# Expert outputs with tokens on partitions and 512 feature columns, and operands placed at the two ends of the on-chip memory

## The chip, the cores and the metric

One core of one Trainium2 chip runs the whole program. Engines are named as the profile names them: PE (TensorE matmul), PEld (its weight load), DVE (VectorE), ACT (ScalarE), POOL (GpSimd), SP (SyncE, which issues nearly all DMAs). The metric is the device time of one execution in microseconds; lower is better.

## The reference: two transformer blocks

256 tokens of 1,024 features go through two blocks in float32. The part that the change touches most is the feed-forward part of the first block, a mixture over 16,384 experts, each with one input row `u` and one output row `v`:

```
s = q . sub_keys;  pick 16 experts for each of 8 heads of each token, gate = softmax(best_s)
u_sel = u[expert];  v_sel = v[expert]
act = gelu(einsum('nd,ned->ne', hx, u_sel))
return einsum('ne,ned->nd', gate * act, v_sel)
```

Around it stand a block with selected attention, pooling branches and `w_out`, and a second block (a recurrent branch, a sparse attention, and a gated feed-forward of width 3,072). The rest is products of a 1,024-wide activation with weight matrices.

## The kernel before, in words

All large products run in float32r with both operands split in two: `x = h + l`. `h` is a rounded copy (ACT), `l` the rest (DVE or POOL), and a product is the sum of three matmuls, h·h, h·l and l·h. Weights arrive in units of 128 x 1,024 float32 (512 KB, one DMA on SP into one of four `raw` buffers). `weights()` hands out a unit and `prefetch()` keeps up to four ready: ACT writes `wh` (L166), DVE or POOL `wl` (L167). The order of units is one list, `stream`, from the first projection to the last one (`w1`, `wup1`, `wout1`, `wpq`, 128 of `u`, 128 of `v`, `w2`, `wup2`, `wout2`, `wff`, `wdn`), so PE goes from one stage to the next on weights that are already split. A unit's `wh` and `wl` stand in a *room*, and a pattern of letters says which: `w` is two pairs of buffers that live through the kernel, the other letters are places free in one stage only. In the u stage the pattern is `wwcc` (units 2 to 60), from the 64th `v` on it is `d`, and from `w2` to the end `wwe`.

Activations lie with features on partitions. `mm3` (L190) multiplies a unit with them: the weight block is loaded into PE (128x128), and 256 tokens stream past (the *moving* operand). A unit is 24 matmuls of 256 columns.

The experts are computed densely. **u stage** (128 units): `h2` (two halves of 128x8x256) streams past each unit, and gelu goes to `actA` or `actB`. After 64 units a second piece of work runs along: `gate_batch` builds for 8 tokens the 0/1 matrices of the chosen experts (four to five DVE operations, `eqa`, `a2`, `b8`), PE multiplies them (16 short matmuls, L797), and DVE multiplies the result into the activations (L805). **v stage** (128 units): ACT and DVE split two rows of activations into `pr` (h and l, L849 and L850), and L854 multiplies: the `v` block of 128 experts x 128 features is loaded, 256 tokens stream:

```
for d in range(8):
    for n, (wl, al) in enumerate(((0, 0), (0, 1), (1, 0))):
        mm = T.matmul(vo[d // 2][:, d % 2], (u.l if wl else u.h)[:, d], pr[al][:, i % 2], ...)
```

The sum of all 128 units stays in four banks of PSUM (`vo`, features on partitions). The first 58 units share the stage with the second half of the gate batches, and every eighth later unit with one `ada` product on DVE. After the last unit DVE adds `vo` into `x` chunk by chunk (L890), ACT and DVE split it into `hb` (L268, L269), and PE starts the first three units of `w2` on each chunk as it comes.

Where tiles lie is decided by pools that grow from the left (low bytes of a partition) or from the right. In the program before, in bytes of a partition: `w` rooms 47,264 to 63,648; `hb` and `mix2` 63,648 to 80,032; `h2` 80,288 to 96,672, and later `pr` in the same place; `oh` and `hf` 94,368 to 110,752; `c` rooms 147,424 to 163,808; `d` rooms (`spare`) 163,808 to 188,384; `ff` 163,808 to 212,960; `hh` and `hl` 212,832 to 229,344; `e` room 221,152 to 229,344. These tiles start 32 bytes past a multiple of 64. *Near* below means under 131,072, *far* above. Rows of activations are 1,024 bytes long, but those of `hh` and `hl` 1,032.

Of the kernel before, what the change touches and what calls it, by code (L numbers as in the profile page):

```python
# [58 lines left out]
def tile_kernel(ctx: ExitStack, tc: tile.TileContext, I, out):  # L59
    nc = tc.nc  # L60
    V, S, G, T = nc.vector, nc.scalar, nc.gpsimd, nc.tensor

    const = ctx.enter_context(tc.tile_pool(name="const", bufs=1))
    rawp = ctx.enter_context(tc.tile_pool(name="rawp", bufs=4))
# [210 lines left out]
    def load_c(wpool_):  # L275
        t = wpool_.tile([128, 1024], F32, name="cb", bufs=1)
# [61 lines left out]
    with ExitStack() as ph:  # L338
# [3 lines left out]
        wpx = pool(hst, "wpx", 2, side="right")  # L342
# [6 lines left out]
        rooms["a"], rooms["b"] = Room(6, wps), Room(2, wpx)  # L349
# [295 lines left out]
        hst = ExitStack()  # L645
        h2p = pool(hst, "h2p", side="left")
# [125 lines left out]
        def gate_batch(hf, act, n0, pg):  # L772
# [10 lines left out]
            a2 = pab.tile([128, 8, 2, 64], F16, name="a2")  # L783
# [4 lines left out]
            b8 = pab.tile([128, 8, 128], BF, name="b8")  # L788
# [23 lines left out]
        for i in range(64):  # L812
            if i == 0:
                pactA = pool(rst, "pactA", side="right")
                actA = [(0, pactA.tile([128, 24, 256], F32, name="actA0", tag="A0")),
# [20 lines left out]
        hst.close()  # L836
        upst.close()
        pp = pool(lst, "pp", 2, side="left")
        vst = ExitStack()
        pv = pool(vst, "pv", side="right", space=PSUM)  # L840
        vo = [pv.tile([128, 2, 256], F32, name=f"vo{i}") for i in range(4)]
        cb = load_c(pp)
        n0 = 0
        for i in range(128):
            u = weights("v", i)
            if i % 2 == 0:
                src = row(actA if i < 64 else actB, i % 64, 2)
                pr = (pp.tile([128, 2, 256], F32R, name="prh"), pp.tile([128, 2, 256], F32R, name="prl"))
                S.activation(pr[0], src, AF.Copy)  # L849
                V.tensor_tensor(pr[1], src, pr[0].bitcast(F32), OP.subtract)  # L850
            first = None
            for d in range(8):
                for n, (wl, al) in enumerate(((0, 0), (0, 1), (1, 0))):
                    mm = T.matmul(vo[d // 2][:, d % 2], (u.l if wl else u.h)[:, d], pr[al][:, i % 2],  # L854
                                  start=(i == 0 and n == 0 and d % 2 == 0),
                                  stop=(i == 127 and n == 2), skip_group_check=True)
                    if i == 0 and n == 0:
                        if d % 2 == 0:
                            first = mm
                        else:  # L860
                            tc.add_manual_dep(mm.ins, first.ins.name, no_sync(), reason="bank start")
# [676 lines left out]
```

## Time and profile before

| | |
|---|---|
| median of 3 runs | 1599.18 us (1594.93 to 1600.08) |
| profiled execution, its own time | 1595.43 us |
| its span in the trace | 1593.0 us |
| PE busy | 1539.8 us, 97%, 13,278 matmuls |
| PE weight loads | 1498.1 us, 94% |
| DVE / ACT / POOL busy | 1278.1 / 834.4 / 211.3 us |
| HBM read | 278.97 MB, 176 GB/s over the span |

A matmul's end in the trace is modelled and successive ones overlap, so a busy PE is not a PE at its peak: what a matmul costs in a stream is read from the distance between starts. In a timeline row such as `1561.77 1.12 PE ... x8` the first number is the start of the first of eight, and the next row's start minus it, over eight, is that distance.

### The profile page before, as it was taken

The numbers are of one execution on the slowest core, as the hardware profiler recorded it, in microseconds if no ns is written. First come the engines' busy times: TensorE is split into PE (matmuls) and PEld (weight loads), VectorE is DVE, ScalarE is ACT, GpSimd is POOL, SyncE is SP. The second block draws the span as 40 slices with busy tenths as digits, with TensorE's granted clock in tenths as the row PEclk, the third lists the DMA queues.
The fourth block names the chain that finished last, engine by engine and source line by source line (L and its number), as shares of the span: only waits on it lengthen the run. The fifth ranks groups of instructions, "written<-read, shape, count | busy, mean of one in ns | idle before, by whom it ended". The sixth has DMA issues, their size and how long they took to land.

```text
span 1593.0 us, 32813 instructions
## 1 busy us (share of the span) xinstructions
PE 1539.8 (97%) x13278; PEld 1498.1 (94%) x13278; DVE 1278.1 (80%) x2437; ACT 834.4 (52%) x1451; POOL 211.3 (13%) x156
## 2 busy tenths in 40 slices
PE   4999998999999999999999999988999999999999
PEld 3989998999999999999999999987888889999999
DVE  8889899984788887999856656888977666799963
ACT  3555563445444445434444444566776664576642
POOL 0100136895000000000000000125000000111100
PEclk9999999999999999999999999989999999999999
DMA  8678543655555555545466666544333335555554
GB/s 312 242 251 289 173 147 134 207 173 190 164 168 162 170 169 176 167 165 170 162 211 211 200 212 218 191 164 133 128 105 110 96 120 170 175 185 186 186 195 123
DMA packets 78215, 283.19 MB, mean 178 GB/s; under 512 B 8680, under 2 KB 9968, under 8 KB 77808
## 3 DMA queue, kind: packets, MB, share of 16 engines
q1 hardware_dynamic: 78064, 281.10, 53.3%
q8 instruction: 104, 1.70, 0.5%
q14 instruction: 47, 0.39, 0.1%
HBM read 278.97 MB, written 2.10 MB: 176 GB/s over the span
## 4 chain that ended last, share of the span: by engine, by line
PE 74%; DVE 6%; ACT 1%; issue 1%; DMA 0%; POOL 0%; ACTq 0%; POOLq 0%; DVEq 0%
PE mm L190 43%; PE vo L854 22%; PE gt L797 2%; DVE wl L167 2%; PE npo L1295 2%; PE pgt L1022 1%; PE npo L1298 1%; PE phd L1062 1%; DVE ri L1088 1%; PE npt L1286 0%; ACT wh L166 0%; DVE ri L1078 0%; DVE xt L992 0%; DVE hrr L946 0%; DVE eq L721 0%
## 5 line engine op out<-in xcount | busy, mean ns | idle before, releaser
L166 ACT ACTIVATE wh<-raw 128x1024 fp32r<-128x1024 f32 x409 | 432.5, 1060 | 471.4 <-PE mm L190 245.8
L167 DVE TENSOR_TENSOR wl<-raw,wh 128x1024 fp32r<-128x1024 f32 x359 | 447.8, 1249 | 104.0 <-ACT wh L166 102.4
L854 PE MATMUL vo<-prh,spare 128*128 128x256 f32 x1024 | 181.1, 281 | 0.0
L854 PEld LDWEIGHTS vo<-prh,spare 128*128 128x128 f32 x1024 | 158.1, 190 | 0.0
L190 PE MATMUL mm<-h2h,wl 128*128 128x256 f32 x1024 | 143.6, 283 | 5.7 <-DVE wl L167 5.7
L854 PE MATMUL vo<-prh,wh 128*128 128x256 f32 x512 | 146.7, 288 | 0.2 <-ACT prh L849 0.2
L190 PE MATMUL mm<-h2h,wh 128*128 128x256 f32 x1024 | 146.3, 286 | 0.0
L854 PE MATMUL vo<-prl,wh 128*128 128x256 f32 x512 | 144.5, 283 | 0.1
L854 PE MATMUL vo<-prh,wl 128*128 128x256 f32 x512 | 144.3, 283 | 0.2 <-DVE wl L167 0.2
L256 POOL TENSOR_TENSOR r<-r,sq 128x256 f32<-128x256 f32 x18 | 14.6, 809 | 978.0 <-DVE kh L960 606.7
L190 PE MATMUL mm<-h2l,wh 128*128 128x256 f32 x1024 | 144.0, 284 | 0.0
L854 PE MATMUL vo<-prl,spare 128*128 128x256 f32 x512 | 143.9, 281 | 0.0
L167 POOL TENSOR_TENSOR wl<-raw,wh 128x1024 fp32r<-128x1024 f32 x50 | 134.8, 2717 | 66.8 <-ACT wh L166 39.7
L190 PEld LDWEIGHTS mm<-h2h,wl 128*128 128x128 f32 x1024 | 131.8, 192 | 6.3 <-DVE wl L167 6.3
L190 PEld LDWEIGHTS mm<-h2l,wh 128*128 128x128 f32 x1024 | 132.3, 192 | 0.0
L190 PEld LDWEIGHTS mm<-h2h,wh 128*128 128x128 f32 x1024 | 131.2, 191 | 0.2
L167 DVE TENSOR_TENSOR spare<-raw,spare 128x1024 fp32r<-128x1024 f32 x64 | 78.4, 1225 | 65.5 <-ACT spare L166 65.5
L166 ACT ACTIVATE spare<-raw 128x1024 fp32r<-128x1024 f32 x64 | 67.8, 1059 | 92.3 <-PE vo L854 89.5
L854 PEld LDWEIGHTS vo<-prl,wh 128*128 128x128 f32 x512 | 98.0, 191 | 0.2 <-DVE prl L850 0.2
L854 PEld LDWEIGHTS vo<-prh,wl 128*128 128x128 f32 x512 | 97.8, 191 | 0.4 <-DVE wl L167 0.4
L854 PEld LDWEIGHTS vo<-prh,wh 128*128 128x128 f32 x512 | 97.8, 191 | 0.3 <-ACT prh L849 0.3
L854 PEld LDWEIGHTS vo<-prl,spare 128*128 128x128 f32 x512 | 96.1, 188 | 0.0
(419 smaller groups left out, 3270.5 us busy)
## 6 DMA issues: line engine op xcount, KB each, us to landing
raw<-in_u_dram SPq DMA_DIRECT2D x128, 512.0 KB, 3.6
raw<-in_v_dram SPq DMA_DIRECT2D x128, 512.0 KB, 3.6
raw<-in_w_dram SPq DMA_DIRECT2D x86, 512.0 KB, 4.3
raw<-in_wada_dram SPq DMA_DIRECT2D x48, 512.0 KB, 4.9
raw<-in_wff_dram SPq DMA_DIRECT2D x48, 512.0 KB, 4.3
raw<-in_wup_dram SPq DMA_DIRECT2D x27, 512.0 KB, 3.6
raw<-in_wdn_dram SPq DMA_DIRECT2D x24, 512.0 KB, 4.4
raw<-in_wout_dram SPq DMA_DIRECT2D x16, 512.0 KB, 3.7
```

What stands on the lines that cost most here:

```text
L166: S.activation(u.h, t, AF.Copy)
L167: (G if n in on_pool and on_pool[n](i) else V).tensor_tensor(u.l, t, u.h.bitcast(F32), OP.subtract)
L190: T.matmul(ps, (u.l if wl else u.h)[:, s], a[al][:, k], start=start and n == 0, stop=stop and n == len(seq) - 1)
L256: eng.tensor_tensor(tot, tot, sq, OP.add)
L797: mm = T.matmul(ps[:, t], b8[:, t], a2[:, t, s], start=(t == 0 and s == 0), stop=(s == 1), skip_group_check=True)
L854: mm = T.matmul(vo[d // 2][:, d % 2], (u.l if wl else u.h)[:, d], pr[al][:, i % 2], start=(i == 0 and n == 0 and d % 2 == 0), stop=(i == 1 ...
L1022: T.matmul(ps[:pn], w[:kn, idx % 8, :pn], a[:kn, i], start=(j == 0 and n == 0), stop=(j == len(ins) - 1 and n == 2))
L1062: T.matmul(phd, cw[hf][:, l], cb[:, 8 * hf + l], start=(hf == 0 and l == 0), stop=(hf == 1 and l == 7))
L1088: V.tensor_tensor_scan(ri[:, m], ra[:, m], xc[:, m], 0.0, op0=OP.mult, op1=OP.add)
L1295: T.matmul(po[64 * s:64 * s + 64], vs[i // (b + 1)][:, i % (b + 1), 64 * g:64 * g + 64], pT[:, s, i], start=(i == 0), stop=False)
L1298: T.matmul(po[64 * s:64 * s + 64], vc[:15, g], ct[:15, 2 * hp + s], start=False, stop=True)
```

## The change

**v stage.** The operands change sides. Now 128 tokens of `pr` are loaded into PE, and 512 feature columns of `wh`, `wl` or `spare` stream past. A unit is 12 matmuls of 512 columns instead of 24 of 256, in the order of the terms. `vo` holds tokens on partitions. The products of the last two units are ordered so that the first 512 features are complete before the second. Then ACT and DVE copy `vo` to `vt` (two copies of 128x512 each), PE turns it in 16 transposes of 128x128 into the same banks, and L928 adds it to `x`.

**Places.** A pool `hot` of 16 KB at the far end (212,928 to 229,312) holds in turn the `b` rooms, `h2`, three sets of `pr`, `hb` and `mix2`. `oh` and `hf` move to 196,544 to 212,928, `ff` to 139,200 to 188,352. The `d` rooms move near (80,384 to 104,960), the `e` room too (63,744 to 71,936). The `c` rooms stay far (155,584 to 171,968), the `w` rooms near (47,360 to 63,744). Two pad tiles make these tiles start at multiples of 64 bytes. `a2` and `b8` become one tile, and the row `c` for the last `ada` products is loaded at the 64th unit of `v` into a buffer of that pool instead of at the start of the stage.

```
+    const.tile([128, 24], F32, name="near_pad")
+    far_pad.tile([128, 8], F32, name="far_pad")
...
+    hot = ctx.enter_context(tc.tile_pool(name="hot", bufs=1, reuse_waits="tile", side="right"))
+    def hot_acts(name):
+        t = hot.tile([128, 2, 8, 256], F32R, name=name, tag="hot")
+        return t[:, 0], t[:, 1]
...
+        pA0 = pool(lst, "pA0", side="left")
-        h2 = (h2p.tile([128, 8, 256], F32R, name="h2h"), h2p.tile([128, 8, 256], F32R, name="h2l"))
+        h2 = hot_acts("h2")
...
+        pv_ = hot.tile([128, 8, 2, 256], F32R, name="pr", tag="hot")
+        prs = [(pv_[:, 2 * n], pv_[:, 2 * n + 1]) for n in range(3)]
...
+        vo = [[pv.tile([128, 4, 128], F32, name=f"vo{b}{hf}") for hf in range(2)] for b in range(2)]
+        def v_products(halves):
+            for u, pr, i in held_v:
+                for n, (wl, al) in enumerate(((0, 0), (0, 1), (1, 0))):
+                    for b in range(2):
+                        for hf in halves:
+                            T.matmul(vo[b][hf], pr[al][:, i % 2, b * 128:b * 128 + 128],
+                                     (u.l if wl else u.h)[:, 4 * hf:4 * hf + 4],
+                                     start=(i == 0 and n == 0), stop=(i == 127 and n == 2))
...
+            held_v.append((u, pr, i))
+            if i < 126:
+                v_products(range(2))
+                held_v.clear()
+            elif i == 127:
+                for hf in range(2):
+                    v_products([hf])
...
-                spare = pactA.tile([128, 3, 2, 8, 128], F32R, name="spare", tag="A0")
+                spare = pA0.tile([128, 3, 2, 8, 128], F32R, name="spare", tag="A0")
-        rooms["e"] = Room(1, pool(ctx, "wpe", 1, side="right"))
+        rooms["e"] = Room(1, pool(ctx, "wpe", 1, side="left"))
-        hb = (b2h.tile([128, 8, 256], F32R, name="hbh", tag="hbh"),
-              b2h.tile([128, 8, 256], F32R, name="hbl", tag="hbl"))
+        hb = hot_acts("hb")
...
+        for hf in range(2):
+            S.activation(vt[0][:, 4 * hf:4 * hf + 4], vo[0][hf], AF.Copy)
+            V.tensor_copy(vt[1][:, 4 * hf:4 * hf + 4], vo[1][hf])
+        def turned(m):
+            t = vo[m % 4 // 2][m // 4][:, 2 * (m % 2):2 * (m % 2) + 2]
+            for b in range(2):
+                T.transpose(t[:, b], vt[b][:, m], ident)
+            return t.rearrange("p b n -> p (b n)")
+        yo = [turned(m) for m in range(4)]
         for m in range(8):
+            if m < 4:
+                yo.append(turned(4 + m))
-            xm = V.scalar_tensor_tensor(x[:, m], vo[m // 2][:, m % 2], ada[:, 40 + m:41 + m], x[:, m],
+            xm = V.scalar_tensor_tensor(x[:, m], yo[m], ada[:, 40 + m:41 + m], x[:, m],
...
-        b2o = pool(ctx, "b2o", side="left")
+        b2o = pool(ctx, "b2o", side="right")
```

PE in the middle of the v stage, before (each `vo` is one bank that holds two chunks of 128 features; a unit is eight such triples):

```order
L854 MATMUL vo_8091<-prh,wh 128x256
L854 MATMUL vo_8091<-prl,wh 128x256
L854 MATMUL vo_8091<-prh,wl 128x256
L854 MATMUL vo_8091<-prh,wh 128x256
L854 MATMUL vo_8091<-prl,wh 128x256
L854 MATMUL vo_8091<-prh,wl 128x256
L854 MATMUL vo_8092<-prh,wh 128x256
```

And PE with the change, one whole unit (`vo_8020` and `vo_8021` are the two feature halves of the first 128 tokens, `vo_8022` and `vo_8023` of the others; `pr` stands for its h and its l):

```order
L865 MATMUL vo_8020<-wh,pr 128x512
L865 MATMUL vo_8021<-wh,pr 128x512
L865 MATMUL vo_8022<-wh,pr 128x512
L865 MATMUL vo_8023<-wh,pr 128x512
L865 MATMUL vo_8020<-wh,pr 128x512
L865 MATMUL vo_8021<-wh,pr 128x512
L865 MATMUL vo_8022<-wh,pr 128x512
L865 MATMUL vo_8023<-wh,pr 128x512
L865 MATMUL vo_8020<-wl,pr 128x512
L865 MATMUL vo_8021<-wl,pr 128x512
L865 MATMUL vo_8022<-wl,pr 128x512
L865 MATMUL vo_8023<-wl,pr 128x512
```

Twelve long matmuls stand where 24 short ones stood, and `wl` is first needed at the ninth of twelve instead of at the third of 24.

DVE at the end of the v stage, before (the `x` rows add the expert output, the `hbl` rows split it):

```order
L890 SCALAR_TENSOR_TENSOR x<-vo_8091,ada,x 128x256 x2
L890 SCALAR_TENSOR_TENSOR x<-vo_8092,ada,x 128x256
L958 MEMSET nought 128x4
L1058 COPY cb<-vec 128x16 x2
L960 CAST kh<-nought 128x4
L167 TENSOR_TENSOR wl<-raw,wh 128x1024
L269 SCALAR_TENSOR_TENSOR hbl<-x,vec,hbh 128x256 x3
```

And DVE with the change:

```order
L179 TENSOR_TENSOR wl<-raw,wh 128x1024 x2
L915 COPY vt_11234<-vo_8022 128x512
L915 COPY vt_11234<-vo_8023 128x512
L928 SCALAR_TENSOR_TENSOR x<-vo_8020,ada,x 128x256 x2
L928 SCALAR_TENSOR_TENSOR x<-vo_8022,ada,x 128x256
L281 SCALAR_TENSOR_TENSOR hb<-x,vec,hb 128x256
```

Two copies stand ahead of the first `x`, and the split of a weight unit that stood between `x` and `hbl` stands ahead of both. On PE, 16 transposes (L921) stand between the last product of `v` and the first of `w2`.

## Rows read from the trace of the kernel before

**Rows 1.** Windows: each engine's busy time (operations), granted clock, DMA share, GB/s

```profile
288.00:405.00 117.00, 116.98 (x985) 116.98 (x986) 86.83 (x205) 55.44 (x84) 88.46 (x33) 1.00 0.59 194
414.00:614.00 200.00, 200.00 (x2035) 198.62 (x2034) 166.90 (x287) 85.21 (x127) 0.00 (x0) 1.00 0.51 167
616.00:802.00 186.00, 185.87 (x1897) 184.46 (x1896) 174.22 (x294) 79.46 (x91) 0.00 (x0) 1.00 0.51 168
802.00:998.00 196.00, 195.84 (x1660) 195.62 (x1660) 117.40 (x134) 93.32 (x108) 0.00 (x0) 1.00 0.67 212
1013.00:1300.00 287.00, 272.87 (x2109) 251.13 (x2108) 231.30 (x471) 196.51 (x479) 34.82 (x33) 0.97 0.38 124
1300.00:1384.00 84.00, 83.53 (x690) 81.19 (x689) 57.84 (x85) 42.98 (x69) 4.48 (x6) 1.00 0.53 176
1384.00:1523.00 139.00, 138.56 (x1161) 138.31 (x1160) 129.85 (x216) 95.93 (x146) 17.74 (x24) 1.00 0.57 183
```

**Rows 2.** Chain that ended last, v stage: start, us, what

```profile
640.77 5.82 PE vo L854 x48
646.59 0.48 PE gt L797 x16
```

**Rows 3.** Tile vo: duration min/median/max, first and last start

```profile
L854 PE MATMUL vo<-prh,spare x1024: 281/281/283, 817.2 to 998.0; 128*128 128x256 f32 x171
```

**Rows 4.** Timeline of PE, last stage, units in `e`, `w`, `w`, `e`

```profile
1561.77 1.12 PE L190 MATMUL mm<-ffh,wh 128*128 128x256 f32 x8
...
1564.65 1.07 PE L190 MATMUL mm<-ffh,wh 128*128 128x256 f32 x8
...
1567.37 1.07 PE L190 MATMUL mm<-ffh,wh 128*128 128x256 f32 x8
...
1570.09 1.12 PE L190 MATMUL mm<-ffh,wh 128*128 128x256 f32 x8
```

**Rows 5.** Timeline of PE, u stage, units in `w`, `c`, then `w`

```profile
340.30 1.12 PE L190 MATMUL mm<-h2h,wh 128*128 128x256 f32 x8
...
343.18 1.11 PE L190 MATMUL mm<-h2h,wh 128*128 128x256 f32 x8
...
348.83 1.12 PE L190 MATMUL mm<-h2h,wh 128*128 128x256 f32 x8
```

**Rows 6.** Timeline of PE, `wff` stage, a unit in `e`, then `w`

```profile
1451.32 1.11 PE L190 MATMUL mm<-hfh,wh 128*128 128x256 f32 x8
...
1454.15 1.12 PE L190 MATMUL mm<-hfh,wh 128*128 128x256 f32 x8
```

**Rows 7.** Timeline of PE, first projection, one unit in `w`, then the next

```profile
117.14 1.11 PE L190 MATMUL mm<-hh,wh 128*128 128x256 f32 x8
...
119.98 1.12 PE L190 MATMUL mm<-hh,wh 128*128 128x256 f32 x8
```

**Rows 8.** Timeline of PE at 114 us, three windows: plain float32, two passes a matmul

```profile
114.36 0.91 PE L507 MATMUL pl<-kk,q 64*128 64x256 f32 x3
...
114.36 1.13 PE L507 MATMUL pl<-kk,q 64*128 64x256 f32 x4
...
114.68 0.81 PE L507 MATMUL pl<-kk,q 64*128 64x256 f32 x3
```

**Rows 9.** Timeline of weight loads, ahead of matmuls of 2 columns

```profile
64.23 1.41 PEld L226 LDWEIGHTS ms<-blk,sq 128*128 128x128 f32 x12
65.57 0.19 PEld L190 LDWEIGHTS mm<-hh,wh 128*128 128x128 f32 x1
```

**Rows 10.** Timeline at the end of the v stage

```profile
996.19 1.27 DVE L890 SCALAR_TENSOR_TENSOR x<-vo,ada,x 128x256 f32<-128x256 f32 x3 [1.28 <-PE vo L854]
...
997.99 0.28 PE L854 MATMUL vo<-prh,spare 128*128 128x256 f32 x1
...
1000.68 0.39 PE L190 MATMUL mm<-hbl,wh 128*128 128x256 f32 x1 [2.05 <-DVE hbl L269]
```

**Rows 11.** Timeline of DVE, v stage: an operation of 128x512 from PSUM

```profile
704.42 0.69 DVE L805 SCALAR_TENSOR_TENSOR actB<-gt,actB 128x512 f32<-128x512 f32 x1 [0.54 <-PE gt L797]
```

More of the change, by code (lines that the diff above doesn't have):

```diff
@@ L348, in tile_kernel @@
         wps = pool(stp, "wps", 6, side="left")
-        rooms["a"], rooms["b"] = Room(6, wps), Room(2, wpx)
+        wpx = hot.tile([128, 2, 2, 8, 128], F32R, name="wpx", tag="hot")
+        rooms["a"] = Room(6, wps)
+        rooms["b"] = Room(2, pairs=[(wpx[:, n, 0], wpx[:, n, 1]) for n in range(2)])
         sqrt_next()
@@ L782, in gate_batch @@
                             i1b[:, sl, None].to_broadcast([128, 8, 32, 2]), OP.is_equal)
-            a2 = pab.tile([128, 8, 2, 64], F16, name="a2")
+            ab = pab.tile([128, 2, 1024], BF, name="ab")
+            a2 = ab[:, 1].bitcast(F16).rearrange("p (t s i) -> p t s i", t=8, s=2)
             for s in range(2):
@@ L835, in tile_kernel @@
                 n0 += 8
-        hst.close()
         upst.close()
-        pp = pool(lst, "pp", 2, side="left")
+        pv_ = hot.tile([128, 8, 2, 256], F32R, name="pr", tag="hot")
+        prs = [(pv_[:, 2 * n], pv_[:, 2 * n + 1]) for n in range(3)]
         vst = ExitStack()
         pv = pool(vst, "pv", side="right", space=PSUM)
-        vo = [pv.tile([128, 2, 256], F32, name=f"vo{i}") for i in range(4)]
-        cb = load_c(pp)
+        vo = [[pv.tile([128, 4, 128], F32, name=f"vo{b}{hf}") for hf in range(2)] for b in range(2)]
+        cb = None
         n0 = 0
+        held_v = []
+        def v_products(halves):
[6 more added lines that the diff above has]
+                                     start=(i == 0 and n == 0), stop=(i == 127 and n == 2))
         for i in range(128):
@@ L847, in tile_kernel @@
                 src = row(actA if i < 64 else actB, i % 64, 2)
-                pr = (pp.tile([128, 2, 256], F32R, name="prh"), pp.tile([128, 2, 256], F32R, name="prl"))
+                pr = prs[i // 2 % 3]
                 S.activation(pr[0], src, AF.Copy)
                 V.tensor_tensor(pr[1], src, pr[0].bitcast(F32), OP.subtract)
[L851 to L861, printed above, removed]
+            held_v.append((u, pr, i))
[5 more added lines that the diff above has]
+                    v_products([hf])
             if i < 64:
@@ L888, in tile_kernel @@
         los = []
+        vtp = pool(vst, "vtp", side="right")
+        vtp.tile([128, 4096], F32, name="gap")
+        vt = [vtp.tile([128, 8, 128], F32, name=f"vt{b}") for b in range(2)]
+        for hf in range(2):
[7 more added lines that the diff above has]
+        yo = [turned(m) for m in range(4)]
         for m in range(8):
-            xm = V.scalar_tensor_tensor(x[:, m], vo[m // 2][:, m % 2], ada[:, 40 + m:41 + m], x[:, m],
+            if m < 4:
+                yo.append(turned(4 + m))
+            xm = V.scalar_tensor_tensor(x[:, m], yo[m], ada[:, 40 + m:41 + m], x[:, m],
                                         op0=OP.mult, op1=OP.add)
@@ L1366, in tile_kernel @@
         yw = pool(ph, "yw", 2, side="right")
-        mix = (b2h.tile([128, 8, 256], F32R, name="mix2h", tag="hbh"),
-               b2h.tile([128, 8, 256], F32R, name="mix2l", tag="hbl"))
+        mix = hot_acts("mix2")
         for m in range(8):
```

13 lines of the change are left out of this document (6 added, 7 removed).

## The prediction

> **What bounds the kernel now.** [...] DVE comes close in the first v window (174.2 of 186 us) and in `wff` (129.9 of 139) [rows 1]. [...]
>
> [...] In the last stage, whose activations lie far, the three units from 1561.77 us on start at 1561.77, 1564.65, 1567.37 and 1570.09: 24 matmuls take 2.88 us where the weights lie far (120.0 ns each) and 2.72 us where they lie near (113.3 ns) [rows 4]. The other engines do the same work around all three. In the u stage, activations near, the unit with near weights takes 2.88 us (120 ns) and two with far weights 5.65 us (117.7 ns) [rows 5]. `wff`, activations near too, repeats it: 2.83 us with far weights, 117.9 ns [rows 6]. The second part of v, pr near and weights far, 64 units of 24 matmuls, runs at (998.0 - 817.2) / 1536 = 117.7 ns [rows 3]. So four cases: both near 120, both far 120, activations near and weights far 117.7, activations far and weights near 113.3.
>
> A weight load by itself, ahead of matmuls of two columns, takes (1.41 - 0.19) / 11 = 111 ns [rows 9]. That is nearly the whole distance at 256 columns. The nearest stream that lasts longer is plain float32 at 256 columns: the fourth pass adds 1.13 - 0.91 = 0.22 us to three, and the last two of three add (0.81 - 0.38) / 2 = 0.215 (a single one lasting 0.38 by 1.13 less three distances), so 216 ns; but the first pass of a pair takes 114.68 - 114.36 = 0.32 [rows 8]. I have no row of a 512-column float32r matmul.
>
> **The change, part by part.** (1) *512 columns.* The 3,072 matmuls of v become 1,536. [...] Bounds: 216 below; above, twice the short ones, 227 to 240 ns [rows 4, 5]. The first 58 units share PE with 32 gate batches of 0.48 us [rows 2]: 58 x 12 x 0.216 = 150.3, plus 15.4, plus the 3.6 that today's 186 holds over 58 x 24 x 0.120 + 15.4, is 169 us. But DVE has 174.2 us of work there, which the change leaves as it is, so it becomes the limit: I take 175, a gain of **11 us** and not 17 [rows 1]. The other 70 units: 70 x 12 x 0.216 = 181.4 against 196, gain **14.6**; DVE (117) and ACT (93) stay under it, and the DMAs, 0.67 of their time busy now, would go to 0.72 [rows 1].
>
> (2) *Activations far, weights near* (6.7 ns a matmul against both near, 4.4 against far weights). *u stage, second part*: 64 units, 1,523 matmuls in the window, x 6.7 = **10.2 us**; DVE's 166.9 of 200 still fits in 190 [rows 1]. *u stage, first part*, 288 to 405 us: half of the 41 units gain 6.7 ns, the half in `c` rooms, now far with `h2` far, loses 2.3 (120 against 117.7): 492 x 6.7 - 492 x 2.3 = **2.2 us**; POOL, 88.5 / 33 = 2.68 us per `wl`, stays just under a unit's mean of 2.80 [rows 1]. Before 288 us I count nothing: what streams there (`hh`, `hl`) was far before and stays so. *w2 stage*: 1,320 matmuls, two in three in `w` rooms (6.7) and one in three in the `e` room (4.4), make 7.8; DVE is busy 231 of 287 us there and PE waits for it in places, so I take **5**, between 0 and 7.8 [rows 1]. *wup2 and wout2*: 384 with `oh` and `mix2` at a mean of 5.9 ns gain 2.3; the 264 on `y`, near as before, lose 2.3 ns in the `e` room, 0.2: **2.1**. *wff*: 1,152 x 5.9 = **6.8**, which brings the window to 132 against DVE's 129.9: just under [rows 1]. *wdn*: 192 matmuls in the `e` room x 6.7 = **1.3** [rows 4]. Is far enough? The new place, from 212,928 up, was held only by `hh`, whose unit with near weights takes 2.84 us (118.3 ns) [rows 7]; its rows are 1,032 bytes apart, those of `h2`, `pr`, `hb` and `mix2` 1,024 as in `ff`, so I go by `ff`, with 118.3 as the other bound.
>
> (3) *Multiples of 64.* No row has both operands on one. All of 113, 118 and 120 are read 32 bytes past. [...] I take nothing.
>
> (4) *End of v.* Today 2.7 us pass from the last expert matmul to PE's first on `hbl`, 2.05 of them a wait [rows 10]. With the change DVE copies the second half (0.69, as an operation of 128x512 from PSUM takes [rows 11]), then three `x` (1.27 for three [rows 10]) and one `hb` (some 0.45, as `x`): 2.4 us and two passages between engines, about the same. The 16 transposes need 16 weight loads of 0.111 = 1.8 us [rows 9], inside that wait; without it they would cost their 1.8. The remaining `x` and `hb` come a little later than today, because today three `x` are done before the last matmul: **cost 1 us**, 0 to 4. What is queued behind the second copy on DVE is every `x`, and PE waits for these. Its late start delays nothing but the first three units of `w2`.
>
> (5) *The row `c`* is now loaded at the 64th unit, ahead of a `raw` load that already makes DVE wait; the `d` rooms hold three units ahead. One `a2`/`b8` tile instead of two keeps two buffers. `pr` has three sets for two. The `b` rooms, `h2`, `pr`, `hb`, `mix2` follow each other in one place, each after a stage that PE runs in order. I price these at 0; the cover is the units kept ready.
>
> Sum: 11 + 14.6 + 10.2 + 2.2 + 5 + 2.1 + 6.8 + 1.3 - 1 = **52.2 us** off the profiled execution's 1595.43, or 1543.2. That execution is 3.75 us under the median of 1599.18, so a median of about **1547**.
>
> **The rivals.**
>
> *Places do nothing for PE.* Then 113.3 comes from something else in the last stage. Left are 25.6 of (1) less 1: **1575**. The alternation inside one stage speaks against it [rows 4, 6]; `hh` at 118.3 speaks for a part of it [rows 7]. [...]
>
> [...]
>
> *Long streams cost more than 216.* At 227 the 70 units take 190.7 and the first 58 177: 40.9 us gained in all, **1558**. At 240 the 70 take 201.6 and the 58 take 186: 21 gained, **1578**.
>
> *Slower: the weight load is not hidden behind long streams.* The 0.32 us of a first float32 pass is 216 plus a load of about 107 [rows 8, 9]. Were every matmul of v like it, v would take 1536 x 0.32 + 19 = 511 us against 382, and the kernel **1700**. It decides from 254 ns on, where 1536 of them use up the other 26.6 us. Against it: at 256 columns the load is hidden today, or the distance would be over 200 ns [rows 3].
>
> *The change does not do what it says:* the waits of (5), or DVE in the two near-full stages, give back what PE saves, and the time is within a few us of today, **1595 to 1605**.
>
> **How the numbers follow.** Forecast (1540 to 1559) 0.58; alignment gives more 0.17; places do nothing 0.08; long streams at 227 to 240 0.08; given back 0.06; load not hidden 0.03. Within 0.3% of 1599, 4.8 us, is about what a measurement can't tell from no change. The first four cases are faster: 0.91. Given back divides 0.04 same and 0.02 slower, and the last adds 0.03: slower 0.05. The range reaches from 1524, the fast end of alignment, to 1577, which takes in "places do nothing" and most of the long streams; about 0.12 is left out.
>
> **What would show it.** L865's distance near 216 ns in the second part of v; 24 matmuls of `h2` on `w` rooms in 2.72 us or less, and 2.88 in `c` rooms; DVE filling the first part of v with PE waiting for it; the wait at the end of v about as long as today; `wff` with DVE over 0.95. Wrong would be: a distance over 227 ns in v, or `h2` at 118 to 120 in its new place.

## The result, and the profile after

| | before | after |
|---|---|---|
| median | 1599.4 us (1594.9 to 1600.1) | 1572.2 us (1571.4 to 1573.8) |
| ratio, 95% interval | | 0.984 (0.9822 to 0.9858) |
| profiled execution, its span | 1593.0 us | 1570.0 us |
| `u`, first to last start | 395.1 us | 390.4 us |
| `v` | 382.7 us | 369.3 us |
| last product of `v` to first of `w2` | 0.1 us | 2.1 us |
| `wff` | 138.4 us | 136.7 us |
| `wdn` | 66.7 us | 67.7 us |

The change is worth 27 us where 52 were forecast. The two profiled executions differ by 23.0 us in their spans, and the forecast was summed against the one of before. The windows by stage (columns as in [rows 1]) of the changed kernel:

```profile
414.00:608.00 194.00, 194.00 (x2060) 192.86 (x2060) 168.66 (x289) 85.32 (x129) 0.00 (x0) 1.00 0.55 176
611.00:799.00 188.00, 188.00 (x1232) 151.04 (x1230) 179.50 (x301) 85.76 (x100) 0.00 (x0) 1.00 0.54 175
799.00:978.00 179.00, 179.00 (x784) 146.87 (x783) 110.78 (x124) 86.65 (x98) 0.00 (x0) 1.00 0.70 227
1362.00:1498.00 136.00, 135.46 (x1150) 135.22 (x1149) 132.61 (x212) 91.70 (x145) 17.69 (x24) 1.00 0.58 186
```

PE fills these four stretches, or nearly, as it filled those of [rows 1], at a granted clock of 1.00, so what counts is the distance between starts. In v the tile's view (columns as in [rows 3]) gives it: from 804.0 to 979.6 us lie 767 steps, 228.9 ns each, where 216 were forecast.

```profile
L865 PE MATMUL vo<-spare,pr x768: 388/392/396, 804.0 to 979.6; 128*128 128x512 f32 x192
L865 PE MATMUL vo<-wh,pr x512: 388/392/502, 610.3 to 802.9; 128*128 128x512 f32 x171
```

For 256 columns I read PE's timeline: two units of `u` in `w` rooms and one in a `c` room (336 to 345 us), one unit late in `u`, and one unit of `wff`:

```profile
336.42 2.05 PE L202 MATMUL mm<-h,wh 128*128 128x256 f32 x16
...
339.25 2.05 PE L202 MATMUL mm<-h,wh 128*128 128x256 f32 x16
...
342.08 2.08 PE L202 MATMUL mm<-h,wh 128*128 128x256 f32 x16
...
344.96 1.24 PE L202 MATMUL mm<-h,wh 128*128 128x256 f32 x9
...
595.55 1.98 PE L202 MATMUL mm<-h,wh 128*128 128x256 f32 x16
...
598.27 1.98 PE L202 MATMUL mm<-h,wh 128*128 128x256 f32 x16
...
1402.70 1.10 PE L202 MATMUL mm<-hfh,wh 128*128 128x256 f32 x8
...
1405.52 1.10 PE L202 MATMUL mm<-hfh,wh 128*128 128x256 f32 x8
```

From one row shown to the next is a unit of 24 matmuls. At 336 us the `w` rooms take 2.83 us a unit (117.8 ns) and the `c` room 2.88 (120). At 595 us the same `w` rooms with the same `h2`, no address changed, take 2.72 (113.3). `wff` takes 2.82 to 2.83 throughout, and so does `wdn`, where `w` rooms had 2.72 before [rows 4]. So the places alone do not give 113.3.

The view of waits shows PE standing in the first part of `u` for splits that queue on DVE behind the top-k (us in total, times, longest), first before the change, then with it:

```profile
PE mm L190 <- DVE wl L167: 5.7, 3, 3.6
...
PE mm L202 <- DVE wl L179: 8.3, 3, 4.1
```

The end of v, in the timeline:

```profile
979.59 1.92 PEld L921 LDWEIGHTS vo<-ident,vt 128*128 128x128 f32 x16
...
980.02 0.69 DVE L915 COPY vt<-vo 128x512 f32<-128x512 f32 x1 [1.33 <-PE vo L865]
...
980.63 1.26 DVE L928 SCALAR_TENSOR_TENSOR x<-vo,ada,x 128x256 f32<-128x256 f32 x3
...
981.70 1.02 PE L202 MATMUL mm<-hb,wh 128*128 128x256 f32 x4
...
982.34 0.19 PEld L202 LDWEIGHTS mm<-hb,wh 128*128 128x128 f32 x1 [0.22 <-DVE hb L281]
```

The first product on the low half of `hb`, whose load is the last row, comes 2.8 us after the last product of v (979.56), against 2.7 before [rows 10]. The transposes fill what was a wait. The first product on the high half comes 2.1 us after it instead of 0.1.

### The profile page after: what moved, and what is told of

Same layout as the page of the kernel before. It is cut to its first block, busy times and chain, and to the rows that moved or that the text cites. A ratio compares the mean times of both kernels' runs of the same rounds, so it can differ in the third digit from the quotient of the medians.

```text
span 1570.0 us, 29771 instructions
## 1 busy us (share of the span) xinstructions
PE 1514.9 (96%) x11758; PEld 1404.7 (89%) x11758; DVE 1286.6 (82%) x2439; ACT 831.3 (53%) x1453; POOL 213.6 (14%) x156
## 5 line engine op out<-in xcount | busy, mean ns | idle before, releaser
L202 PE MATMUL mm<-h,wh 128*128 128x256 f32 x2048 | 263.8, 282 | 0.0
L202 PEld LDWEIGHTS mm<-h,wh 128*128 128x128 f32 x2048 | 249.5, 191 | 0.2
L865 PE MATMUL vo<-spare,pr 128*128 128x512 f32 x768 | 176.0, 391 | 0.0
L865 PEld LDWEIGHTS vo<-spare,pr 128*128 128x128 f32 x768 | 144.2, 188 | 31.6
L202 PE MATMUL mm<-h,wl 128*128 128x256 f32 x1024 | 141.9, 282 | 8.3 <-DVE wl L179 8.3
L202 PEld LDWEIGHTS mm<-h,wl 128*128 128x128 f32 x1024 | 129.9, 192 | 8.9 <-DVE wl L179 8.9
L202 PE MATMUL mm<-hb,wh 128*128 128x256 f32 x928 | 130.7, 287 | 0.6 <-ACT wh L178 0.2
L865 PE MATMUL vo<-wh,pr 128*128 128x512 f32 x512 | 130.8, 397 | 0.3 <-ACT pr L874 0.3
L202 PEld LDWEIGHTS mm<-hb,wh 128*128 128x128 f32 x928 | 117.6, 192 | 3.7 <-issue 1.4
L865 PEld LDWEIGHTS vo<-wh,pr 128*128 128x128 f32 x512 | 93.7, 188 | 19.0 <-ACT pr L874 0.4
```

Of the source, the lines that this page charges most:

```text
L202: T.matmul(ps, (u.l if wl else u.h)[:, s], a[al][:, k], start=start and n == 0, stop=stop and n == len(seq) - 1)
L865: T.matmul(vo[b][hf], pr[al][:, i % 2, b * 128:b * 128 + 128], (u.l if wl else u.h)[:, 4 * hf:4 * hf + 4], start=(i == 0 and n == 0), stop ...
```

## Experiments: what each part is worth

Three parts can be put in singly: the **turn** of v to 512 columns, the two **pads**, and the **places** (far activations, near rooms). Five kernels leave out one or two of them. `x_turn_only` is the kernel before with the new v stage:

```
-        vo = [pv.tile([128, 2, 256], F32, name=f"vo{i}") for i in range(4)]
+        vo = [[pv.tile([128, 4, 128], F32, name=f"vo{b}{hf}") for hf in range(2)] for b in range(2)]
...
+                            T.matmul(vo[b][hf], pr[al][:, i % 2, b * 128:b * 128 + 128],
+                                     (u.l if wl else u.h)[:, 4 * hf:4 * hf + 4],
```

> The kernel before with the 512-column v stage and its turning at the end alone; every place as before (pr near, w rooms near in the first part of v, spare far in the second). Kernel before: 1599.4 us, v 382.7 us. Theory 1 (a long matmul takes twice a short one on the same places): 240 ns in the first part, where both operands lie near, and 227 to 236 in the second; v 375 to 389 us, the end of v 2 us longer, total 1594 to 1607. Rival 2 (the long stream costs 229 ns wherever its operands lie): v 369 us as in the changed kernel, total 1586 to 1589.

`x_pads_only` is the kernel before with

```
+    const.tile([128, 24], F32, name="near_pad")
+    far_pad = ctx.enter_context(tc.tile_pool(name="far_pad", bufs=1, side="right"))
+    far_pad.tile([128, 8], F32, name="far_pad")
```

> The kernel before with the two pad tiles alone: all its tiles start at multiples of 64 bytes, in the order and the places of before. Kernel before: 1599.4 to 1600.5 us. Theory 1 (a multiple of 64 sets no distance of 256-column matmuls; only the rhythm that they fall into may change): u at 120, v at 120 and 117.7, total within 4 us of 1600. Rival 2 (alignment is worth what the changed kernel loses without the pads, 1584 against 1572, 12 us): total 1588 to 1592, with a shorter distance in v.

`x_turn_pads` has both of these edits:

> The kernel before with the 512-column v stage and the two pads, all places as before: what is missing to the changed kernel is the move of activations and rooms alone. The turn alone gave 1584.9 us, the pads alone 1591.4, the changed kernel 1572.2. Theory 1 (the places are worth little of their own, since 113.3 is only one of two rhythms of operands that lie apart, and the second part of u is the one long stretch that keeps it): v 366 to 370 us, u 393 to 397, total 1577 to 1582, so 5 to 10 us for the places. Rival 2 (the places carry the 25.6 us that the prediction gave them): total 1595 to 1600. Rival 3 (they carry nothing, turn and pads are all): 1571 to 1574.

`x_no_pads` takes the three pad lines out of the changed kernel:

> The changed kernel without its two pad tiles: every tile starts 32 bytes past a multiple of 64 again, the far and near places are kept to within 96 bytes. Theory 1 (a multiple of 64 does nothing for PE): the distances stay at 113.3 in the second part of u, 229 in v, 117.8 in wff, and the total within 3 us of 1572.2. Rival 2 (it does): the distance in the second part of u goes back to 117.7 to 120, total 1579 to 1583; or wff and wdn go to 113.3 as the last stage had before, total 1564 to 1567. DVE operations may change too: an operation of 128x2048 in the first part of u was 4.4 us before and 2.3 or 9.2 with the change.

`x_v256` undoes the turn in the changed kernel and keeps its places:

```
-                            T.matmul(vo[b][hf], pr[al][:, i % 2, b * 128:b * 128 + 128],
-                                     (u.l if wl else u.h)[:, 4 * hf:4 * hf + 4],
+                    mm = T.matmul(vo[d // 2][:, d % 2], (u.l if wl else u.h)[:, d], pr[al][:, i % 2],
```

> The changed kernel with the v stage as it was before (24 matmuls of 256 columns a unit, weights loaded, pr streams, no turning at the end), all places kept: pr far, weight rooms near. Changed kernel: 1572.2 us, v stage 369.3 us from its first matmul to its last. Theory 1 (the 512-column form brings nothing of its own: its 229 ns is twice a short matmul of operands that lie apart, and v became faster because pr moved away from the weights): 256 columns at 113.3 ns where a gate batch interrupts the stream and 113.3 to 117.8 ns where nothing does, so v takes 361 to 374 us, the 2 us between v and w2 go, total 1562 to 1577. Rival 2 (the long stream is what made v faster): 256 columns at 117.7 to 120 ns as before, v 378 to 383 us, total 1579 to 1584.

Measured (the ratio is to runs of the kernel before on the same chip; the last two columns are spans between first starts in one profile each):

| kernel | turn | pads | places | median, us | ratio (95%) | `u` | `v` |
|---|---|---|---|---|---|---|---|
| before | | | | 1599.4 | 1 | 395.1 | 382.7 |
| `x_turn_only` | x | | | 1584.9 | 0.992 (0.9891 to 0.995) | 397.2 | 368.4 |
| `x_pads_only` | | x | | 1591.4 | 0.9954 (0.9933 to 0.9974) | 395.9 | 376.3 |
| `x_turn_pads` | x | x | | 1586.8 | 0.9937 (0.9916 to 0.9958) | 397.8 | 371.8 |
| `x_no_pads` | x | | x | 1583.9 | 0.9909 (0.9874 to 0.9944) | 392.3 | 375.3 |
| `x_v256` | | x | x | 1575.5 | 0.9861 (0.983 to 0.9892) | 388.4 | 370.1 |
| after | x | x | x | 1572.2 | 0.984 (0.9822 to 0.9858) | 390.4 | 369.3 |

A few us between single profiles say little here: before the first product of `u`, which most of these edits do not touch, the profiles of all runs take between 217.7 and 224.3 us. The turn alone came near rival 2 (v at 368.4), the short matmuls on the new places as theory 1 had it (v at 370), and both runs on the pads on rival 2's side. The parts don't add. The turn is worth 13 us alone (0.8%) and nothing that can be told apart once pads and places are there (0.9861 against 0.984, intervals overlapping). In v each way of its own leads to about 369: `x_turn_only` has the places of before, `x_v256` the short matmuls of before. The reason shows in the tile's view of the second part of v, first `x_v256`, then `x_turn_only`:

```profile
L868 PE MATMUL vo<-pr,spare x1536: 276/276/387, 809.4 to 984.1; 128*128 128x256 f32 x192
```

```profile
L851 PE MATMUL vo<-spare,prh x512: 388/392/397, 809.1 to 984.6; 128*128 128x512 f32 x171
```

`x_v256` takes 1,535 steps in 174.7 us, 113.8 ns. Outside a few waits a unit there takes 2.72 us, 113.3 ns a matmul, and twice that is 226.7. So 512 columns save nothing over two good short matmuls; they save over the 117.7 to 120 ns of before.

The pads, priced at zero, are worth 7 us alone, nothing on top of the turn, and 11 on top of turn and places. The tile's view of the second part of v shows a part of why, first `x_no_pads`, then `x_turn_pads`, then `x_pads_only`:

```profile
L862 PE MATMUL vo<-spare,pr x768: 393/397/398, 807.5 to 986.5; 128*128 128x512 f32 x192
```

```profile
L854 PE MATMUL vo<-spare,prh x512: 393/394/394, 809.7 to 988.7; 128*128 128x512 f32 x171
```

```profile
L857 PE MATMUL vo<-prh,spare x1024: 275/276/281, 822.2 to 996.7; 128*128 128x256 f32 x171
```

With long matmuls a step takes 233.3 ns in `x_no_pads` and again 233.3 in `x_turn_pads`, against 228.9 both in the changed kernel and in `x_turn_only`. So with `pr` far and `spare` near the pads take 4.4 ns off a step, and with `pr` near and `spare` far they add 4.4: rival 2 of `x_turn_only`, 229 ns wherever the operands lie, does not hold in general. With short matmuls `x_pads_only` went from 117.7 [rows 3] to 113.7 on the mean. In `u` the distances changed places: without the pads the `w` units of the first part took 2.72 us and the second part ran at 117.8 ns, where the changed kernel has 2.83 us and 113.3. For 256 columns, then, 113.3 and 117.8 both occur with the pads and without them, and whether 32 bytes act by themselves there, or only something decides between the two, is not shown.

The places on top of turn and pads are worth 0.9937 less 0.984, 15 us, of 27.6 forecast: step (2) of the prediction sums to 27.6, and the 25.6 that rival 2 of `x_turn_pads` names is the forecast gain of the turn. The total of `x_turn_pads` hit none of its three expectations; it lies between theory 1, which gave the places 5 to 10 us, and rival 2, which gave them all.

## Experiment: the distances with nothing else running

`x_probe` adds blocks of 48 matmuls behind the last product of the changed kernel:

```
+        def probe(st, mv, n, reset, off=0, count=48):
+            ps = px.tile([128, 512], F32, name="pr0", tag="x")
+            for _ in range(3 * reset):
+                T.transpose(ps[:, :128], ident, ident)
+            for k in range(count):
...
+                T.matmul(ps[:, :n], st[:, 128 * (k % 8):128 * (k % 8) + 128], mv[:, a:a + n],
+                         start=(k == 0), stop=(k == count - 1))
```

> The changed kernel with 18 blocks of 48 matmuls (the first of 96) added behind its last product, when no other engine works: operands near or far in all four ways, 256 and 512 columns, some blocks after three short transposes, some right behind another block, two with the moving operand 32 bytes further on. Their results go nowhere, the output is that of the changed kernel, and the total says nothing. Theory 1 (PE alone makes the distances: same side 120, apart 113.3 after short matmuls and 117.8 behind a block at 120; 512 columns twice that, 226 to 240): the blocks show these numbers with all other engines idle. [...]

One window of it shows PE alone (columns as in [rows 1]), and PE's timeline the blocks. In these rows `hfh` and `mix` lie far and `wh` near; the first name is the moving operand, and a row with `wh` alone has both near.

```profile
1592.30:1597.00 4.70, 4.70 (x43) 4.70 (x41) 0.00 (x0) 0.00 (x0) 0.00 (x0) 1.00 0.00 0
```

```profile
1569.16 11.04 PE L1475 MATMUL pr<-hfh,wh 128*128 128x256 f32 x96
1580.04 0.49 PE L1472 MATMUL pr<-ident 128*128 128x128 f32 x3
1580.29 5.70 PE L1475 MATMUL pr<-hfh,wh 128*128 128x256 f32 x48
1585.82 5.92 PE L1475 MATMUL pr<-hfh,mix 128*128 128x256 f32 x48
1591.58 5.82 PE L1475 MATMUL pr<-hfh,wh 128*128 128x256 f32 x48
1597.24 0.49 PE L1472 MATMUL pr<-ident 128*128 128x128 f32 x3
1597.48 5.90 PE L1475 MATMUL pr<-hfh,wh 128*128 128x256 f32 x48
1603.22 5.91 PE L1475 MATMUL pr<-wh 128*128 128x256 f32 x48
1608.97 5.63 PE L1475 MATMUL pr<-hfh,wh 128*128 128x256 f32 x48
1614.44 0.49 PE L1472 MATMUL pr<-ident 128*128 128x128 f32 x3
...
1649.95 11.45 PE L1475 MATMUL pr<-hfh,wh 128*128 128x512 f32 x48
1661.24 0.49 PE L1472 MATMUL pr<-ident 128*128 128x128 f32 x3
1661.49 11.16 PE L1475 MATMUL pr<-hfh,mix 128*128 128x512 f32 x48
1672.49 0.49 PE L1472 MATMUL pr<-ident 128*128 128x128 f32 x3
...
1683.73 11.15 PE L1475 MATMUL pr<-wh,mix 128*128 128x512 f32 x48
1694.72 0.49 PE L1472 MATMUL pr<-ident 128*128 128x128 f32 x3
```

Start to next start: apart 10.88 / 96 = 113.3 ns; both far 5.76 / 48 = 120.0; then the same operands as in the first block 5.66 / 48 = 117.9. Both near gave 120 too. At 512 columns both far takes (11.00 - 0.31) / 47 = 227.4, the 0.31 being the first one behind the transposes. Apart it takes 10.99 / 48 = 229.0 with the loaded operand far and the moving one near, as in the changed kernel, and (11.29 - 0.32) / 47 = 233.4 the other way round, as in `x_turn_pads`. The windows read inside seven of these blocks (256 columns apart, both far and both near; 512 apart and both far) show DVE, ACT and POOL at 0.00 us and a DMA share of 0.01 at most, so the distances of these seven need no other engine. Theory 1 stands for the distances, not for what sets them. With the moving operand 32 bytes further on, one block of 256 columns apart took 119.8, and one of 512 took 232.3.

Two rows say what the forecast missed. Apart has two **rhythms**, 113.3 and 117.9, for the same operands. What turns the one into the other does not follow theory 1: behind the first block at 120 (1585.82) came 117.9, behind the second (1603.22) came 5.47 / 48 = 114.0, and the blocks behind three transposes (1580.29 and 1597.48, without their first matmul of 0.20 us 113.4 and 117.9) kept the rhythm of the block ahead of the transposes. And long streams want the opposite of short ones: one side 227, apart 229 to 233.5.

## Experiments: the rhythm inside the kernel

`x_reset` puts three transposes ahead of the third unit of `wff`, `after_again` is the changed kernel once more:

```
+                if m == 1 and i == 0:
+                    for _ in range(3):
+                        T.transpose(ps[:, :128], ident, ident)
```

> The changed kernel with three transposes of 128x128 into the output of the third unit of wff ahead of its first product, which overwrites them; nothing else. In the changed kernel wff and wdn run at 117.8 ns with activations far and weights near, the second part of u at 113.3 with the same places, each unit there starting after some short matmuls. Theory 1 (operands that lie apart allow two rhythms, 113.3 and 117.8 ns, and which one PE keeps is set by what it did just before; short matmuls set it to 113.3): wff from the third unit on and wdn run at 113.3, 1,104 + 576 matmuls x 4.5 ns less 0.4 us: 7 us less, total 1565. Rival 2 (the distance belongs to the addresses): 117.8 stays, total 1572 to 1573.

> The changed kernel once more, unchanged, for a second profile and its time beside the run above. Theory 1 (which of 113.3 and 117.8 ns a stretch keeps is set by small differences in what came before it): at least one of wout2, wff and wdn runs at another of the two distances than in the first profile (113.3, 117.8, 117.8), with every address the same; v again at 229 and the second part of u at 113.3. Rival 2 (each stretch has its distance by its addresses and its program): the same distances as in the first profile. Total 1570 to 1575 in both.

`x_reset`: 1571.2 us, 0.9835 (0.9804 to 0.9865). The rhythm changed as forecast, from the transposes to the end of `wff` and, after a stall, in `wdn`; the time did not. PE's timeline and its waits:

```profile
1403.16 1.07 PE L202 MATMUL mm<-hfh,wh 128*128 128x256 f32 x8
...
1405.88 1.07 PE L202 MATMUL mm<-hfh,wh 128*128 128x256 f32 x8
```

```profile
PE mm L202 <- ACT ffh L223: 3.4, 1, 3.4
```

A unit takes 2.72 us against 2.82 in the changed kernel, and `wff` 132.2 against 136.7 us. But PE then stands 3.4 us at the start of `wdn` for the last chunk of `ff`, and the granted clock is lower around this pause (0.90 from 1495 to 1512 us, 1.00 from 1370 to 1495): `wdn` takes 70.5. What is won is 1.7 of some 7 us.

`after_again`: 1573.5 us, 0.9863 (0.9811 to 0.9915). Its `wout2`, `wff` and `wdn` kept 113.3, 117.8 and 117.8, as in the first profile, which is rival 2's side. But other runs show that the addresses and the instructions ahead don't settle it. `x_probe` is the changed kernel up to its last product, and there `wout2` ran at 117.8 and `wff` at 113.3 (131.7 us, then 3.8 us of wait at the start of `wdn`). In `x_reset` `wout2` ran at 117.8 as well, though its edit stands behind `wout2`.

Nor is it shown that the transposes made the change in `x_reset`. Five kernels have them. In `x_reset` alone the rhythm changed there; in `x_mul_dve` and `x_lean` below it was 117.8 ahead of them and stayed so, in `x_reset_pool` and `x_all` it was 113.3 ahead of them already. 16 short matmuls in `x_lean_b` did not change 117.8 either. What decides the rhythm is left open.

`x_c_near` moves the `c` rooms near, so that nothing in the first part of `u` lies on one side:

```
+        ust = ExitStack()
+        wpu = pool(ust, "wpu", 2, side="left")
...
-                rooms["c"] = Room(2, pool(ust, "wpu", 2, side="right"))
+                rooms["c"] = Room(2, wpu)
```

> The changed kernel with the c rooms near as well (104,960 to 121,344 instead of 155,584 to 171,968; the scratch tiles of the top-k move up by 16 KB); h2 stays far. Changed kernel: in the first part of u two units in w rooms take 2.83 us each and two in c rooms 2.88. Theory 1 (operands on one side always take 120 ns; apart they take 113.3 or 117.8, and a unit that follows one at 120 ns takes 117.8): without units at 120 ns the short matmuls at the start of u set 113.3 and it stays: some 58 units of 2.72 us, 8 us less work for PE; POOL's split of 2.75 us a unit and the stalls behind the top-k give part of it back, so 3 to 6 us less, total 1566 to 1569. Rival 2 (the first part of u has another limit, POOL and the top-k on DVE): units of 2.72 us but more and longer stalls on wl, total 1571 to 1574. Rival 3 (the distance belongs to addresses): 2.83 us in all four rooms, total 1571.

1570.7 us, 0.9827 (0.9795 to 0.9859): no gain to be told from the changed kernel's. PE's timeline shows both rhythms on the same rooms, 2.83 us a unit at 251 and 2.72 at 294; it changed at a stall from 274 us on. The waits of the first part of `u` grew from 8.3 to 12.2 us:

```profile
251.48 2.05 PE L202 MATMUL mm<-h,wh 128*128 128x256 f32 x16
...
254.31 2.05 PE L202 MATMUL mm<-h,wh 128*128 128x256 f32 x16
...
294.65 1.98 PE L202 MATMUL mm<-h,wh 128*128 128x256 f32 x16
...
297.37 1.86 PE L202 MATMUL mm<-h,wh 128*128 128x256 f32 x15
```

```profile
PE mm L202 <- DVE wl L179: 12.2, 3, 4.7
```

So theory 1's distances and rival 2's stalls are both there: a faster PE only reaches the splits behind the top-k earlier. Its `wff` also fell into 113.3 (131.7 us), with 3.8 us of wait at the start of `wdn`, which then took 73.2: all of the gain went back.

`x_same_v` moves the `d` rooms of v far, to the side of `pr`:

```
-            if i == 32:
+            if i == 62:
...
-                spare = pA0.tile([128, 3, 2, 8, 128], F32R, name="spare", tag="A0")
+                spare = pactA.tile([128, 3, 2, 8, 128], F32R, name="spare", tag="A1")
```

> The changed kernel with the d rooms of the second part of v far (171,968 to 196,544) instead of near, so that pr and weights lie on the same side there. With every other engine idle, 48 matmuls of 512 columns took 227.1 to 227.2 ns on one side and 228.9 to 233.5 apart; matmuls of 256 columns the other way round, 120 and 113.3 to 117.8. Theory 1 (for long streams one side is the better place): the second part of v falls from 228.9 to 227.1 ns, 1.5 us over 840 matmuls, total 1570 to 1572. Rival 2 (apart is better for long streams as well, as the prediction had it for short ones): 236 to 240 ns, 6 to 9 us more, total 1578 to 1581.

The tile's view:

```profile
L865 PE MATMUL vo<-spare,pr x768: 387/389/397, 813.4 to 987.3; 128*128 128x512 f32 x192
```

173.9 us for 767 steps, 226.7 ns: one side is better for 512 columns in the kernel too, 1.7 us in v. The total, 1574.8 us (0.9843, 0.9811 to 0.9875), can't show so little.

## Experiments: what takes the gain of `wff` back

At 113.3 ns PE wants two units every 5.44 us. In `x_reset` DVE worked through 1488.62 to 1494.23 us, the start of one pair's group to the next, without a pause: 5.61. `x_reset_pool` relieves it by POOL, `x_mul_dve` takes POOL's own work to DVE; both keep the transposes.

```
-    on_pool = {"u": lambda i: i < 60 and (i % 4 or 22 < i < 42)}
+    on_pool = {"u": lambda i: i < 60 and (i % 4 or 22 < i < 42), "wff": lambda i: i % 6 == 5}
```

> The run with three transposes in wff, and besides every sixth unit of wff is split by POOL instead of DVE (8 of 48). With the transposes alone wff ran at 113.3 ns, two units in 5.44 us, while DVE needed 5.61 for two without a pause; PE then stood 3.4 us at the start of wdn for the last ff chunk, 5.3 us with what followed at the lower clock. Theory 1 (DVE is the limit of wff once PE runs at 113.3): with 8 x 1.2 to 1.7 us less on DVE it keeps up, the stall goes, total 1565 to 1567. Rival 2 (POOL's 2.5 us slow DVE down meanwhile, as in the first part of u): the stall stays or grows, total 1570 to 1574.

```
-            G.tensor_tensor(cv[0], cv[0], cv[1], OP.mult)
+            V.tensor_tensor(cv[0], cv[0], cv[1], OP.mult)
```

> The run with three transposes in wff, and the product of the two halves of the gate (128x256, 24 times) made by DVE instead of POOL. With the transposes alone DVE set the pace of wff: 5.61 us for two units, of which one split took 1.74 us while POOL made that product in 0.74, and the other 1.22. Theory 1 (the wait of DVE for POOL costs more than the product itself): 5.61 less 0.52 plus 0.41, so about 5.5 against PE's 5.44; the stall at the start of wdn shrinks from 3.4 us to under 2 or goes, total 1566 to 1568. Rival 2 (the product is only added to DVE): 6.0 us for two units, wff at 144 us, total 1580.

`x_reset_pool`: 1580.3 us, 0.9884 (0.985 to 0.9918), `wff` at 141.5 us: rival 2's side, and slower than it said. PE waited 5.0 us for POOL's splits, from the first of these waits on it ran for long stretches at 117.8, and 3.7 us of stall at the start of `wdn` stayed. `x_mul_dve`: 1571.5 us, 0.9828 (0.981 to 0.9846). Here `wff` stayed at 117.8 (137.1 us, no stall), so it says nothing of the stall; but product and splits on one engine kept up with that pace.

Three runs leave out one tap of the convolution, to give DVE room:

```
-                for j, d in ((1, 1), (0, 2)):
+                for j, d in ((1, 1),):
```

> The run with three transposes in wff, and one of the two shifted taps of wff's convolution left out (48 operations of 0.5 us on DVE; the output lacks that tap). It shows what wff and wdn take when DVE has room: theory 1 (DVE is all that keeps the shorter distance from paying there): wff about 131 us, wdn 65.3, no stall between, 196.5 in all against 202.8 with the transposes alone and 204.5 in the changed kernel; total 1564 to 1566. Rival 2 (the stall at the start of wdn has another cause, the chain through ACT and POOL behind the last unit): the stall stays above 2 us, total 1569 to 1571.

> The run with the left-out tap of wff's convolution (the output lacks that tap), with 16 short bf16 matmuls of 64 columns, like those of a gate batch, in place of the three transposes ahead of the third unit of wff. Theory 1 (DVE alone keeps the shorter distance from paying in wff): if the short matmuls set 113.3, wff takes about 131 us, wdn 65.3, no stall between them; total about 1564 to 1567. Rival 2 (the stall at the start of wdn comes from the chain through ACT and POOL behind the last unit): a stall over 2 us stays. If wff falls into 117.8 again, this run tells nothing of the stall.

> The kernel with the c rooms near, which held 113.3 ns through all of wff and then stood 3.8 us for the last ff chunk, with one shifted tap of wff's convolution left out (48 operations of 0.5 us on DVE, 1 us of 5.61 for two units; the output lacks that tap). Theory 1 (DVE's 5.61 us for two units against PE's 5.44 is what the stall is made of): wff 131.7 us again, no stall, wdn 65 to 68 us instead of 73.2. Rival 2 (the stall is the chain DVE, ACT, POOL, ACT behind the last unit): it stays above 2 us. If wff falls into 117.8 ns, the run says nothing of it.

1577.3, 1575.3 and 1568.2 us, one execution each. In all three `wff` ran at 117.8 ns (137.1, 137.3 and 136.7 us) without a stall, so none of them tells theory from rival. That DVE alone makes the stall is therefore not shown. What stands for it: the stall came in each of the kernels without `x_mul_dve`'s edit whose `wff` kept 113.3 (3.4 us in `x_reset`, 3.8 each in `x_c_near`, `x_no_pads` and `x_probe`), and it was shorter with that edit in the next one.

## Experiment: what the runs point to, in one kernel

`x_all` has the edits of `x_c_near`, `x_same_v`, `x_reset` and `x_mul_dve`.

> What the runs point to, in one kernel, with nothing left out: c rooms near, d rooms far, three transposes in wff and the gate's product on DVE. If the parts add up: u 2 us less by the near c rooms (388.1 against 390.4 us), v 1.5, wff and wdn 4 to 6: total 1562 to 1566 against 1572.2 for the changed kernel. If POOL's pace, the top-k and DVE take it back as they did one by one: 1568 to 1572.

1563.0 us (1553.9 to 1567.1), ratio 0.9768 (0.9742 to 0.9794): faster than the kernel before and, by intervals that don't touch, than the changed one. The total is inside the range for parts that add up. Its `u` takes 385.4 us against 390.4, nearly all units of the first part at 113.3 but with 12.5 us of waits; v 367.6; `wff` and `wdn` 132.0 and 68.7 against 136.7 and 67.7. A part of this is luck: `wff` was at 113.3 before it came to the transposes, so the edits did not bring that rhythm. The rows of POOL and DVE in `x_reset`, and then of DVE in `x_all`, speak for the product's move to DVE as what shortened the stall:

```profile
1497.77 0.74 POOL L1457 TENSOR_TENSOR cc<-cc,cc 128x256 f32<-128x256 f32 x1 [4.88 <-DVE cc L1453]
```

```profile
1497.85 1.74 DVE L179 TENSOR_TENSOR wl<-raw,wh 128x1024 fp32r<-128x1024 f32 x1
```

```profile
1479.20 0.43 DVE L1458 TENSOR_TENSOR cc<-cc,cc 128x256 f32<-128x256 f32 x1
...
1479.88 1.22 DVE L179 TENSOR_TENSOR wl<-raw,wh 128x1024 fp32r<-128x1024 f32 x1
...
1484.76 0.43 DVE L1458 TENSOR_TENSOR cc<-cc,cc 128x256 f32<-128x256 f32 x1
```

A split that began while POOL was at its product took 1.74 us, 0.52 more than the 1.22 of one while POOL stood idle; on DVE the product costs 0.43, and two units 5.56 us. The wait at the start of `wdn` is 0.9 us here.

## Why the prediction came out at half

The sign and the range held. Of the 29 us missing against the profiled execution, by the prediction's own steps:

**(1) 512 columns: the term that was mis-sized most.** The 216 ns are those of plain float32 at 256 columns [rows 8], and no run shows them at 512 columns of float32r. What the runs showed there is 227 to 233 ns, 229 in the changed kernel, inside the bounds of 216 to 240 that the step itself gave. Units 0 to 57 went from 184.1 to 177.2 us, 6.9 instead of 11, the rest from 198.7 to 192.3, 6.4 instead of 14.6: 12 us. DVE did not become the limit of the first part (179.5 of 188 us busy, PE never idle), because PE did not get fast enough. The prediction's own sign of being wrong, over 227 ns in v, came. The rival "long streams cost more than 216" had this, with 1558 us at 227 ns.

**(2) Places: right where tried longest, wrong as a rule.** The second part of `u` gave 9.0 us of 10.2, at 113.3 ns as forecast. The step that failed is "so I go by `ff`, with 118.3 as the other bound": 113.3 was taken for what far activations and near weights cost, and it is one of two rhythms that they allow. `wff` stayed at 117.8 in both profiles, 1.7 us instead of 6.8, and `wdn` lost the 113.3 it had, 1.0 more instead of 1.3 less. In the first part of `u` the `w` units got 117.8 and the `c` units 120, so the two only swapped, and longer waits on DVE came on top: 4.3 us more instead of 2.2 less. That 113.3 was possible there too `x_no_pads` shows, in the same order of units. `wup2` with `wout2` (1.7 of 2.1) came nearly as priced, `w2` about half: see (4).

**(3) Multiples of 64, taken at nothing,** are worth 7 us alone, nothing on top of the turn and 11 in company. "Alignment gives more", 0.17 among the chances, had the sign, but no run shows the shorter distances that its end of 1524 us needs: no stretch of `u`, v or `wff` went under 113 ns a matmul of 256 columns.

**(4) End of v** had the length right, 2.8 us after 2.7, but its gain and `w2`'s cannot be told apart: PE starts `w2` 2.0 us later, and the wait of 2.05 us that stood inside `w2` [rows 10] is nearly gone. From the last product of v to the last of `w2` it was 298.2 us and is 296.0, so 2.2 where 5 less 1 were forecast. **(5)**, priced at 0, shows no new wait of PE on those tiles over 0.3 us.

The rival "places do nothing" had 1575 us, close to the result, for a reason that is wrong: the places are worth 15 us, and what it kept of the turn is not there. `wff`'s bound, "132 against DVE's 129.9: just under", was too narrow as well: when PE did reach 113.3 ns there, DVE needed 5.61 us for PE's 5.44, and most of the gain went into a stall. What sets the rhythm, and with it the size of (2), stays open.

## What to carry to other kernels

A distance read in one stage need not be the price of a pair of places (the same `w` rooms and `h2` gave 117.8 ns at 336 us and 113.3 at 595): look for the same operands at another time in the same trace before multiplying it. Two remedies for one slow distance (a longer stream, better places) did not add here, 13 us for the turn alone and nothing to be told with places and pads there; price the second on top of the first. Where the second engine was busy 0.93 of the time, DVE in `wff` [rows 1], there was room for 7% at best, so ask first what that engine takes for one unit, with what runs beside it (1.74 us for a split beside POOL's product, 1.22 without).

## What the runs showed of the hardware

In `x_probe`, behind the last product and at a granted clock of 1.00, float32r matmuls on 128x128 weights started every 120.0 ns (256 columns) when both operands lay near or both far, and every 113.3 to 114.0 or 117.9 when they lay apart. At 512 columns they started every 227 ns on one side; apart every 229.0 with the loaded operand far and the moving one near, and 233.4 the other way round. In the kernels without the pads these two changed places, in the second part of v: 228.9 in `x_turn_only` with `pr` near and `spare` far, 233.3 in `x_no_pads` the other way round. Where the border between the sides lies is not measured: the near operands ended at 121,344 at most, the far ones began at 139,200 at least. An offset of 32 bytes of the moving operand gave 119.8 and 232.3, in one block each. A rhythm lasted: in `x_reset` 113.3 held for the 1,100 matmuls from the third unit to the end of `wff`, and in the changed kernel 117.8 held through all of `wff` and `wdn`.
